# The first loads of a large matmul: two blocks of w issued by ScalarE, and one cast shared by two engines

## The chip, the core and the metric

The kernel runs on one core of one Trainium2 chip. A core has five engines, each with its own instruction stream: TensorE (PE in the profile; PEld is its weight load), VectorE (DVE), ScalarE (ACT), GpSimd (POOL) and SyncE (SP). Transfers between HBM and the core's memory are carried by 16 DMA engines; an engine only issues them, and a semaphore tells when one has landed. The metric is the time on the device in microseconds (us), lower is better.

## The reference

```python
B, S, D = 8, 2048, 2048          # x: [8, 2048, 2048] f32, w: [2048, 2048] f32
cs = np.cumsum(x, axis=1)
diff = cs - (cs shifted by one along axis 1, zeros first)
return np.matmul(diff, w).astype(np.float32)
```

The difference of a running sum is `x` again, so what must be computed is `x @ w`: 16384 x 2048 by 2048 x 2048, result in f32.

## The kernel before, in words

The 16384 rows of `x` are taken in 128 tiles of 128 rows. The first four tiles (`PLAIN = 4`) are multiplied in bf16, block by block, as `w` arrives from HBM; in this head of the kernel `w` is also measured (its largest values) and turned into scaled f16 blocks. All other tiles go in groups of four through products with sums and differences of these f16 blocks (fewer products, at the price of additions on VectorE and ScalarE). An order written out by hand (`ORDER`, `END_ORDER`) says how the steps of one group mix with those of the next. The change touches the head alone.

The order of each engine's instructions is fixed by the helper `after(engine, ask)`: what is asked for with it comes behind the last instruction so asked for on the same engine. DMAs issued in `fetch` and `load_x` are asked for directly, and follow the order of the code on SP's queue.

The head, step by step (line numbers are those of the profile):

- `w` is cut into 16 blocks of 128 rows (`ko` = 0 to 15) and two halves of 1024 columns (`h` = 0, 1). `fetch(h, ko)` (L257 to L259) loads one block of one half, 128x1024 f32, 512 KB. `load_x(q, rows)` (L223 to L228) loads a quarter of the columns of `x` (`q`), one tile of 128x512 f32, 256 KB, for each row tile in `rows`.
- The loop at L365 issues, all on SP: `x` rows 0 and 1 of quarter 0, block 0 of `w`, `x` rows 2 and 3, block 1, blocks 2 and 3, the four row tiles of quarter 1, blocks 4 to 7, and so on. Eight semaphores serve these loads in turn, so that a load waits until the one eight places before it has landed.
- `cast_x` (L235, VectorE) casts a pair of row tiles to bf16, 128x1024 at once. `turn_x` (L244, TensorE) transposes it in eight matmuls against a unit matrix into PSUM, and `turned` (L253 VectorE, L251 ScalarE) copies that to `xP`, from where TensorE takes it as weights.
- `cast(h, ko)` (L261 to L267) casts a block of `w` to bf16 into one of seven ring buffers `wb`. For the half `h = 0`, blocks below `EARLY = 2` are cast by ScalarE (L265); all others by VectorE (L267).
- `measure(h, ko)` (L273, ScalarE) takes the sum of absolute values of each row of a block.
- `plain(h, r, ko)` (L304) multiplies row tile `r` by a block: for `h = 0` two matmuls of 128x512 for each of the row tiles 0 to 2 and one for row tile 3, the left and then the right 512 columns of `wb`.
- `dummies` (L353) are matmuls of zeros into PSUM banks that are not yet in use. Eleven of them (`WARM`) stand first on TensorE, five and four more behind the two groups of transposes.

The sequence around the change is this (L371 to L380):

```python
        for a in range(2):
            xb = cast_x(0, [a])
            v = turn_x(xb, a, 6 + a)
            dummies([4 + i % 2 for i in range((5, 4)[a])])
            turned(0, a, v, "dve")
            if a == 0:
                for ko in range(EARLY):
                    cast(0, ko)
            for r in (2 * a, 2 * a + 1):
                plain(0, r, 0)
```

Behind it, blocks 1 to 15 follow: cast, measure, the seven matmuls; before every fourth block the next quarter of `x` is cast, transposed and copied. Then comes the second half of `w`, with the turning of `w` into f16 blocks beside it.

Of the kernel before, what the change touches and what calls it, by code (L numbers as in the profile page):

```python
# [10 lines left out]
def kernel(  # L11
# [6 lines left out]
    nc = tc.nc  # L18
    P = 128
# [6 lines left out]
    NH = N // 2  # L26
    NB = 512
# [15 lines left out]
    EARLY = 2  # L43
# [44 lines left out]
    def after(engine, ask):  # L88
        if engine in last:
            with tc.issue_after(last[engine].ins):  # L90
                said = ask()
        else:
            said = ask()
        last[engine] = said[-1] if isinstance(said, tuple) else said
        return said
# [90 lines left out]
    with ExitStack() as head:  # L186
# [4 lines left out]
        def turn_of(tiles):  # L191
            tiles.append(tiles.pop(0))
            return tiles[-1]
# [62 lines left out]

        def fetch(h, ko):  # L257
            wt = whole[ko % KH][:, ko // KH, h, :]
            nc.sync.dma_start(wt, w[ds(ko * P, P), ds(h * NH, NH)])  # L259

        def cast(h, ko):  # L261
            wt = whole[ko % KH][:, ko // KH, h, :]
            b = wb[h, ko] = turn_of(ring)
            if h == 0 and ko < EARLY:
                after("act", lambda: nc.scalar.copy(b, wt))  # L265
            else:
                after("dve", lambda: nc.vector.tensor_copy(b, wt))  # L267
# [14 lines left out]
        def taken(h, ko):  # L282
            cast(h, ko)
            measure(h, ko)
# [80 lines left out]
        for ko in range(KO):  # L365
            if ko in loads:
                load_x(loads[ko])
            if ko < 2:
                load_x(0, range(2 * ko, 2 * ko + 2))
            fetch(0, ko)  # L370
# [10 lines that stand above are left out]
        measure(0, 0)  # L381
        for ko in range(1, KO - 1):
            if ko >= EARLY:
                cast(0, ko)
            measure(0, ko)
            q = (ko + 1) // KQ
            turning = ko % KQ == KQ - 1
            if turning:
                xb = cast_x(q)
            for r in range(PLAIN):  # L390
                if turning and r in (0, PLAIN - 1):
                    a = r // 2
                    turned(q, a, turn_x(xb, a, 7), "act")
                plain(0, r, ko)
# [3 lines left out]
        for ko in range(AHEAD):  # L398
            fetch(1, ko)
            cast(1, ko)  # L400
# [15 lines left out]
        def bring(ko):  # L416
            fetch(1, ko)
            cast(1, ko)
            measure(1, ko)
            if ko == AHEAD:  # L420
                scale_of_w(0)
            if ko > AHEAD:
                turn_left(1)
            if ko == 10:
                load(PLAIN, 0)
                load(PLAIN, 1)
                weigh(PLAIN)
                scale_of(PLAIN)
            if ko == 11:
                narrow(PLAIN)  # L430
# [905 lines left out]
```

## Time and profile before

| | us |
|---|---|
| median of 3 runs | 1449.84 (1449.72 to 1450.08) |
| span of the profiled execution, first to last instruction | 1447.4 |
| TensorE busy (matmul) | 1437.9 (99%) |
| VectorE busy | 1319.0 (91%) |
| ScalarE busy | 970.5 (67%) |
| GpSimd busy | 43.8 (3%) |

The profiled execution's own time is known by its span alone, 1447.4 us; the timed runs take 2.4 us more than that. The granted clock of TensorE is full (1.000) over the span.

Rows of the profile are read like this. A row of a timeline gives start, duration, engine, line, operation, output <- input, shape and count; in square brackets stand the idle time of the engine just ahead, and what ended it (`<-DMA W<-in_w_dram`: a load into the tile `W` had landed). `SPq` is SP's queue of DMA issues. A row of the chain gives start, duration and what the chain was on at that time. A row of the waits gives who waited for whom: us in total, how many times, the longest. A row of the windows gives the stretch, its length, then for each engine busy time and count, the granted clock, the mean busy share of the 16 DMA engines (above 1 where transfers of one engine overlap), and GB/s. The head loads all its data into one tile, `W`, from `in_w_dram` and `in_x_dram`.

### The profile page before, as it was taken

What the parts mean: (1) busy time and instruction counts of PE and PEld (TensorE: products, weight loads), DVE (VectorE), ACT (ScalarE), POOL (GpSimd) and SP (SyncE); (2) the same over time, 40 slices, a digit from 0 to 9 for tenths busy, and PEclk for the clock granted to TensorE, in tenths of its full rate; (3) what the DMA queues carried; (4) which work ended last, traced back from release to release, by engine and by line L of the source; (5) the groups of instructions that cost most, each with busy time, mean ns of one, the idle gap of its engine ahead of it and who ended that gap; (6) DMA issues with size and microseconds to landing.
All of it is one profiled execution on the core that took longest, in us unless ns stands there. A gap on an engine that the chain in (4) does not pass through costs nothing.

```text
span 1447.4 us, 20191 instructions
## 1 busy us (share of the span) xinstructions
PE 1437.9 (99%) x6686; PEld 651.6 (45%) x6692; DVE 1319.0 (91%) x2310; ACT 970.5 (67%) x1472; POOL 43.8 (3%) x130
## 2 busy tenths in 40 slices
PE   8999999999999999999999999999999999999998
PEld 4444444444444444444444444444444444444443
DVE  4899899999999999999999999999999999999998
ACT  6987566666666776666666667666667766666662
POOL 0011000000000000000000000000000000000000
PEclk9999999999999999999999999999999999999999
DMA  9999788899888898888899888998878998889973
GB/s 363 368 257 298 200 234 232 239 253 253 226 224 239 238 254 245 231 233 236 248 247 232 234 238 233 262 240 234 228 234 240 252 234 239 226 242 248 255 200 127
DMA packets 378199, 351.58 MB, mean 243 GB/s; under 512 B 274800, under 2 KB 274800, under 8 KB 377968
## 3 DMA queue, kind: packets, MB, share of 16 engines
q1 hardware_dynamic: 378096, 350.31, 86.5%
q8 instruction: 52, 0.85, 0.2%
q14 instruction: 51, 0.42, 0.1%
HBM read 150.99 MB, written 134.22 MB: 197 GB/s over the span
## 4 chain that ended last, share of the span: by engine, by line
PE 97%; DMA 2%; DVE 0%; SPq 0%; issue 0%; DVEq 0%
PE b L628 62%; PE b L609 33%; PE b L304 2%; DMA W<-in_w_dram 2%; DMA W<-in_x_dram 0%; DVE c L639 0%; PE b L464 0%; SPq L225 0%; DVE wb L267 0%; SPq L259 0%; DVEq L267 0%; DVEq L639 0%
## 5 line engine op out<-in xcount | busy, mean ns | idle before, releaser
L639 DVE SCALAR_TENSOR_TENSOR c<-b,of,c 128x512 f32<-128x512 f32 x790 | 573.6, 746 | 71.1 <-PE b L628 61.4
L609 PE MATMUL b<-W,x 128*128 128x512 f16 x2144 | 507.1, 379 | 0.0
L636 ACT ACTIVATE c<-b,of 128x512 f32<-128x512 f32 x492 | 312.7, 680 | 220.2 <-PE b L628 113.8
L628 PE MATMUL b<-W,x 128*128 128x512 f16 x1904 | 454.9, 379 | 0.0
L164 ACT ACTIVATE F<-F,of 128x1024 f16<-128x1024 f32 x246 | 282.3, 1148 | 175.6 <-DVE of L144 173.4
L628 PEld LDWEIGHTS <-x 128*128 128x128 f16 x2500 | 244.6, 98 | 295.4 <-issue 1.0
L609 PEld LDWEIGHTS <-x 128*128 128x128 f16 x2144 | 209.7, 98 | 253.3 <-issue 0.5
L125 ACT ACTIVATE waste<-F 128x1024 uint8<-128x1024 f32 x246 | 259.3, 1054 | 8.3 <-DMA F<-in_x_dram 6.2
L628 PEld LDWEIGHTS <-inner 128*128 128x128 f16 x1644 | 160.8, 98 | 194.0
L628 PE MATMUL b<-W,inner 128*128 128x512 f16 x940 | 241.2, 379 | 0.0
L599 DVE TENSOR_TENSOR x<-x,x 128x1024 f16<-128x1024 f16 (+1 forms) x390 | 227.1, 583 | 3.3
L628 PE MATMUL b<-flow,x 128*128 128x512 f16 x584 | 149.9, 379 | 0.0
L628 PE MATMUL b<-inner 128*128 128x512 f16 x472 | 121.1, 379 | 0.0
L955 DVE TENSOR_TENSOR flow<-W 128x2048 f16<-128x2048 f16 x87 | 105.7, 1215 | 0.0
L1053 DVE TENSOR_TENSOR b<-b,c 128x512 f32<-128x512 f32 x116 | 80.4, 693 | 12.7 <-PE b L628 12.7
L150 POOL TENSOR_SCALAR of<-uw,of 128x2 f32<-128x2 f32 x124 | 42.6, 357 | 1299.6 <-DVE of L142 717.1
L955 DVE TENSOR_TENSOR flow<-W,inner 128x2048 f16<-128x2048 f16 x58 | 70.7, 1220 | 0.0
L1046 ACT COPY c<-b 128x512 f32<-128x512 f32 x58 | 33.4, 576 | 51.2 <-PE b L628 51.2
L304 PE MATMUL b<-wb,xP 128*128 128x512 bf16 x234 | 53.2, 379 | 2.2 <-ACT wb L265 1.1
L599 DVE TENSOR_TENSOR inner<-x 128x512 f16<-128x512 f16 x117 | 49.3, 421 | 3.1 <-DMA x<-F 1.0
L1046 ACT COPY b<-b 128x512 f32<-128x512 f32 x87 | 51.2, 589 | 0.2 <-PE b L628 0.2
L599 DVE TENSOR_TENSOR inner<-x,inner 128x512 f16<-128x512 f16 x117 | 49.2, 421 | 2.0
(68 smaller groups left out, 517.5 us busy)
## 6 DMA issues: line engine op xcount, KB each, us to landing
F<-in_x_dram SPq DMA_DIRECT2D x246, 512.0 KB, 5.2
out_dram<-c SPq DMA_DIRECT2D x492, 256.0 KB, 3.0
W<-in_w_dram SPq DMA_DIRECT2D x32, 512.0 KB, 8.4
W<-in_x_dram SPq DMA_DIRECT2D x16, 256.0 KB, 7.8
x<-F SPq DMA_TRANSPOSE x246, 3.4
out_dram<-o SPq DMA_DIRECT2D x5, 256.0 KB, 7.0
out_dram<-wb SPq DMA_DIRECT2D x5, 256.0 KB, 7.0
xP<-in_x_dram SPq DMA_DIRECT2D x1, 1024.0 KB, 6.4
```

What stands on the lines that cost most here:

```text
L125: lambda: nc.scalar.activation(waste, where[t][i], ABS, scale=1.0 / ROW, accum_out=sums_of[t][:, i : i + 1],),
L150: after("pool", lambda: nc.gpsimd.tensor_scalar(u, uw, m, None, MUL))
L164: lambda: nc.scalar.activation(narrowed(t)[:, ds(i * NH, NH)], where[t][i], COPY, scale=s),
L304: lambda: nc.tensor.matmul(ps[r][n], xP[:, r, ko, :], wb[h, ko][:, ds(n * NB, NB)], start=(ko == 0), stop=(ko == KO - 1),),
L599: after("dve", lambda: nc.vector.tensor_tensor(dst.all, p.all, q.all, op))
L609: said = nc.tensor.matmul(to[n], a[k], b[k][:, n, :], start=(first and k == 0), stop=(k == KH - 1), skip_group_check=True,)
L628: said = nc.tensor.matmul(to, a[k], b[k], start=(first and k == 0), stop=(k == 3), skip_group_check=True)
L636: after("act", lambda: nc.scalar.activation(c, p, COPY, scale=u))
L639: after("dve", lambda: nc.vector.scalar_tensor_tensor(c, p, u, c, MUL, ADD))
L955: after("dve", lambda: nc.vector.tensor_tensor(in_twos(to), x, y, op))
L1046: after("act", lambda: nc.scalar.copy(c, p))
L1053: after("dve", lambda: nc.vector.tensor_tensor(t, p, s, ADD))
```

## The change

Two things are changed in two helpers. `fetch` issues the first two blocks of the first half of `w` (`h == 0`, `ko < EARLY`) from ScalarE's queue instead of SP's; both come first in ScalarE's instruction stream. All other loads stay on SP, in their order. `cast` of the first block (`h == 0`, `ko == 0`) is cut by columns: VectorE casts the left 512, ScalarE the right 512. In VectorE's stream its half stands between the copy of the first pair of transposed row tiles and the cast of the second pair. Block 1 is still cast whole by ScalarE.

```diff
         def fetch(h, ko):
             wt = whole[ko % KH][:, ko // KH, h, :]
-            nc.sync.dma_start(wt, w[ds(ko * P, P), ds(h * NH, NH)])
+            if h == 0 and ko < EARLY:
+                after(
+                    "act",
+                    lambda: nc.scalar.dma_start(wt, w[ds(ko * P, P), ds(h * NH, NH)]),
+                )
+            else:
+                nc.sync.dma_start(wt, w[ds(ko * P, P), ds(h * NH, NH)])
 
         def cast(h, ko):
             wt = whole[ko % KH][:, ko // KH, h, :]
             b = wb[h, ko] = turn_of(ring)
-            if h == 0 and ko < EARLY:
+            if h == 0 and ko == 0:
+                sides = [ds(n * NB, NB) for n in range(2)]
+                after("dve", lambda: nc.vector.tensor_copy(b[:, sides[0]], wt[:, sides[0]]))
+                after("act", lambda: nc.scalar.copy(b[:, sides[1]], wt[:, sides[1]]))
+            elif h == 0 and ko < EARLY:
                 after("act", lambda: nc.scalar.copy(b, wt))
             else:
                 after("dve", lambda: nc.vector.tensor_copy(b, wt))
```

## The prediction

> **What bounds the kernel now.** I read the page first, then the chain that ended last for the first 45 us, then the timeline of each engine in the first 15 us, and last the windows for the rates of the DMA engines. The page:
>
> ```profile
> span 1447.4 us, 20191 instructions
> ...
> PE 97%; DMA 2%; DVE 0%; SPq 0%; issue 0%; DVEq 0%
> ```
>
> Nearly all of the span is TensorE's own work; 2% of the chain is DMA, and it lies at the start. The span is 1447.4 us, the median of the timed runs 1449.84 us; the 2.4 us between them lie around the span, and I carry them over unchanged. The chain in order of time shows where the DMA part is:
>
> ```profile
> 2.58 6.41 DMA W<-in_x_dram
> ...
> 9.01 7.81 DMA W<-in_w_dram
> ...
> 25.27 7.82 DMA W<-in_w_dram
> ...
> 33.21 0.71 DVE wb L267
> ...
> 33.96 8.16 PE b L304 x37
> ```
>
> From 2.58 to 33.2 us the chain is a ladder of loads: each rung is a load that SP could issue only when the one eight places before it had landed. From 33.96 us on it is TensorE alone. So the end moves by as much as the start of the piece at 33.96 us moves: this is the only place in which the change can earn or lose time, as long as TensorE has no waits of its own later. To move it, two things must both be early: block 12 of `w` (the cast at 33.21 us), and TensorE's work of blocks 0 to 11.
>
> The queue of SP, the only one that loads here:
>
> ```profile
> 0.72 0.87 SPq L225 DMA_DIRECT2D W<-in_x_dram  x2
> 1.65 0.42 SPq L259 DMA_DIRECT2D W<-in_w_dram  x1
> 2.11 0.91 SPq L225 DMA_DIRECT2D W<-in_x_dram  x2
> 3.06 2.29 SPq L259 DMA_DIRECT2D W<-in_w_dram  x3
> 5.39 3.28 SPq L225 DMA_DIRECT2D W<-in_x_dram  x4
> ```
>
> One issue takes about 0.46 us of SP (1.65 to 2.11). How the 16 DMA engines fare (the last two columns are their busy share and GB/s; the first numbers are the stretch and TensorE's busy time):
>
> ```profile
> 2.00:7.00 5.00, 4.37 (x21) 1.86 (x20) 2.29 (x7) 0.00 (x0) 0.00 (x0) 1.00 0.86 252
> ...
> 12.00:33.00 21.00, 19.23 (x114) 9.22 (x115) 10.68 (x16) 17.76 (x29) 0.00 (x0) 1.00 1.04 402
> 11.24:33.96 22.72, 20.88 (x127) 10.17 (x130) 11.80 (x17) 18.78 (x31) 0.00 (x0) 1.00 1.04 402
> ```
>
> In the steady part the engines are full: share 1.04, 402 GB/s. From 2 to 7 us they move 252 GB/s. That is a loss of 5.00 x (1 - 252/402) = 1.87 us of full-rate transfer, and the ladder carries it down to 33.2 us. It has two parts: the engines were less busy, 5.00 x (1 - 0.86/1.04) = 0.87 us, and while busy they moved less, the remaining 1.00 us.
>
> When the loads landed is seen from who waited for them. VectorE (pairs of `x` by L235, blocks of `w` by L267), then ScalarE (blocks 0 and 1 of `w`, L265):
>
> ```profile
> 5.17 0.69 DVE L235 CAST W<-W 128x1024 bf16<-128x1024 f32 x1 [1.91 <-DMA W<-in_x_dram]
> 6.58 0.69 DVE L253 COPY xP<-b 128x1024 bf16<-128x1024 bf16 x1 [0.72 <-PE b L244]
> 9.08 0.69 DVE L235 CAST W<-W 128x1024 bf16<-128x1024 f32 x1 [1.81 <-DMA W<-in_x_dram]
> 10.49 0.69 DVE L253 COPY xP<-b 128x1024 bf16<-128x1024 bf16 x1 [0.72 <-PE b L244]
> 11.57 0.69 DVE L267 CAST wb<-W 128x1024 bf16<-128x1024 f32 x1 [0.39 <-DMA W<-in_w_dram]
> 12.85 0.70 DVE L267 CAST wb<-W 128x1024 bf16<-128x1024 f32 x1 [0.58 <-DMA W<-in_w_dram]
> ```
>
> ```profile
> 0.72 1.28 ACT L265 ACT_TABLE_LOAD   x1 [0.72 <-PEq L1320]
> 7.67 1.04 ACT L265 CAST wb<-W 128x1024 bf16<-128x1024 f32 x1 [5.67 <-DMA W<-in_w_dram]
> 10.28 1.04 ACT L265 CAST wb<-W 128x1024 bf16<-128x1024 f32 x1 [1.57 <-DMA W<-in_w_dram]
> ```
>
> Each of these is 512 KB. They land at 5.17 (`x` rows 0 and 1), 7.67 (`w` 0), 9.08 (`x` rows 2 and 3), 10.28 (`w` 1), 11.57 and 12.85 us. The steady distance is 12.85 - 11.57 = 1.28 us; `w` 0 took 2.50 us behind the first pair. So the loss sits in the first pair and in `w` 0. TensorE in the same stretch:
>
> ```profile
> 1.17 4.11 PE L353 MATMUL b<-F 128*128 128x512 bf16 x11 [1.17 <-DVE F L207]
> 5.92 0.62 PE L244 MATMUL b<-eye,W 128*128 128x128 bf16 x8 [0.63 <-DVE W L235]
> 6.38 1.24 PE L353 MATMUL b<-F 128*128 128x512 bf16 x5
> 8.76 1.02 PE L304 MATMUL b<-wb,xP 128*128 128x512 bf16 x4 [1.14 <-ACT wb L265]
> 9.83 0.62 PE L244 MATMUL b<-eye,W 128*128 128x128 bf16 x8
> 10.29 1.03 PE L353 MATMUL b<-F 128*128 128x512 bf16 x4
> 11.24 1.47 PE L304 MATMUL b<-wb,xP 128*128 128x512 bf16 x6
> ```
>
> From 11.24 us on it has real work without fillers. Its waits between there and 33.96 us, in all:
>
> ```profile
> PE b L244 <- DVE W L235: 0.9, 2, 0.5
> PE b L304 <- DVE wb L267: 0.7, 1, 0.7
> ```
>
> That is 1.6 us (the window 11.24:33.96 above agrees: 22.72 - 20.88 = 1.84, dispatch gaps included). TensorE is thus nearly bound too: work that starts up to 1.6 us later than 11.24 us can still be caught up by 33.96 us, and if it does not start earlier, no more than 1.6 us can be won.
>
> **The change part by part.** *SP loses two issues.* The built program has SP issue the four `x` loads in a row, then blocks 2 and 3. At 0.46 us each, `x` rows 2 and 3 go out at about 1.65 and 2.11 instead of 2.11 and 2.58, and blocks 2 and 3 end at about 3.5 instead of 4.4 us.
>
> *ScalarE gains two issues*, ahead of its table load and of everything else. The trace shows no issue from ScalarE; the nearest rows are SP's 0.42 to 0.46 us, and I take 0.46. They would run from 0.72 to 1.6 us, and the table load to 2.9 us. Nothing on ScalarE wants to run before its first cast (7.67 us before), so this costs nothing; if that cover were gone, it would cost 0.9 us. `w` 0 goes out about 0.9 us sooner (1.65 to 0.72), `w` 1 about 1.9 us sooner (3.06 to 1.2).
>
> *The ladder's waits are renumbered.* The fifth to eighth `x` load now wait for `w` 0, `x` 0, `x` 1, `w` 1 to land, blocks 4 and 5 for `x` 2 and `x` 3. By 3.5 us 2.5 MB and more are in flight, over 6 us at 402 GB/s; SP's in-order wait for `w` 0 finds the engines with work for longer than `w` 0 can take (it landed at 7.67 us before, and it now leaves sooner). Cost nothing; if `w` 1 landed after 9 us, later rungs would slip by the excess.
>
> *The engines' start-up loss* is what decides. The trace shows no second queue at work, so I bound it by rows. At best all of the 1.87 us comes back: everything that was slow is waiting, and two queues wait beside each other. At worst nothing comes back, or `w` 1 takes as long as `w` 0 did: 2.50 - 1.28 = 1.22 us lost. I take the part in which the engines were not busy, 0.87 us: a second queue with a megabyte on offer fills empty time, while the slower transfer of busy engines need not change. This is the value near the middle of the ends, and nearest to a row.
>
> *The cast of `w` 0 is halved.* ScalarE's 1.04 us becomes about 0.57 (between half of it, 0.52, and the whole), VectorE gets one of about 0.4 us (between 0.35, half of 0.69, and 0.69). TensorE's first real matmul may come some 0.5 us sooner after `w` 0 has landed. But what follows at 9.83 us waits for the second pair of `x`, and what is late at 33.21 us is a load. Worth nothing at the end. What it adds is a wait: VectorE now stands at its half until `w` 0 has landed, and behind it are the cast of the second `x` pair and the second copy of L253. That costs only if `w` 0 lands after that pair, which the 0.9 us head start speaks against; then it would cost the difference.
>
> *After 33.96 us* the programs agree instruction for instruction on every engine, except for names and a few semaphore numbers. VectorE's, ScalarE's and SP's work there hangs on TensorE's or on loads of the same ladder, and moves with them.
>
> **Sum:** the loads reach block 12 0.87 us sooner. TensorE's start: with `x` sharing the engines with `w` I expect the first pair at about 6 us. From the pair's landing the rest is VectorE's and TensorE's chain: 2.10 us to the end of the first copy (5.17 to 6.58 + 0.69), 0.37 for VectorE's half, 0.69 for the second cast, and 1.45 to the first matmul behind the second copy, with 0.35 lost to TensorE's own order; about 5 us, so 11.0 us against 11.24. With 1.6 us of slack that suffices. 1449.84 - 0.87 = 1448.97, say 1449.0 us.
>
> **The rivals.** *Only the issue time.* The chain of the ladder starts behind SP's five issues; with one slot of 0.46 us less ahead of the last `x` load, it gains 0.46 us: 1449.4 us. For it: the engines' share of 0.86 leaves little room, and both queues feed the same engines. Against it: 252 GB/s is far from full. If the start-up loss were of the engines alone, even this goes and the time stays at 1449.8. [...] No run here shows two queues yet.
>
> *`x` starves behind `w` (slower).* If the engines serve both queues in turn, and a row of `w` is 4 KB against 2 KB of `x`, `w` gets two bytes for one of `x`. Were the total rate no better than before, the first pair of `x` would land with a megabyte of `w`, 1.5 MB in all, which had landed at 9.08 us before. Then the chain gives about 9.08 + 5.0 = 14.0 us for TensorE's start, 2.8 us later, of which 1.6 can be caught up: 1.2 us slower, 1451.0 us. It decides from a landing of the first pair at 7.9 us. TensorE would also idle from 5.28 to 9.8 us; were it to run the next stretch as slowly as its first eleven matmuls (4.11 us, against 11 x 0.25 = 2.7 by the 1.24 us for five), 1.4 us more: 1452.4. Against it: this needs the low total rate and the uneven share together; at 402 GB/s the pair lands by about 6. [...]
>
> *All of it comes back.* 1.87 us by the loads, but TensorE allows 1.6 and what its start gains: 1448.0 to 1448.2. For it: `w` 0 was slow while busy, and if that is a wait for first accesses it can overlap with `x`. Against: nothing in the trace shows overlap.
>
> **How the numbers follow.** Forecast (0.6 to 1.3 us gained) 0.42; issue time only or nothing (0 to 0.6) 0.23; all of it (1.3 and more) 0.15; `x` starves (0 to 3 us lost) 0.17; something else in the 1400 us behind, either way, 0.03. The likeliest gives 1449.0 us. The range takes in the first three and the near half of the fourth: 1447.8 to 1450.4. About 0.2%, 2.9 us, is what a measurement of this kernel can tell from no change; nearly every case is smaller than that. Faster by more needs more than the whole start-up loss: 0.02. Slower by more needs the starved `x` and the slow TensorE together: 0.04. Within: 0.94.
>
> **What would show it.** In the changed profile, the window 2 to 7 us should have a busy share near 1.0 and some 300 GB/s. The second pair's cast should start before 8.7 us, the cast of block 3 (12.85 us before) near 12.0, that of block 12 near 32.3, and TensorE's first matmul of the long unbroken piece (33.96 before) near 33.1, with nothing but this shift behind it. Wrong would be: a first pair after 7.9 us, a VectorE half that waits for `w` 0 while the second pair lies there, block 3 no sooner than 12.6, or a shift at 33 us that is gone by 130 us.

## The result, and the profile after

The changed kernel takes 1451.97 us (median of 21 runs, 1450.96 to 1452.72), the kernel before beside it 1449.56 us (21 runs). The ratio is 1.0016, with a 95% interval of 1.0009 to 1.0022: 2.4 us slower. The prediction was 0.9 us faster, with a range that ended at 1450.4 us; the time lies outside it. The profiled execution has a span of 1450.5 us (1447.4 before) and took 1452.44 us; it is one of the slower of the 21, so its span grows by 3.1 us where the medians differ by 2.4.

The timelines show what became of the loads. VectorE of the changed kernel, from the cast of the first pair of `x` on:

```profile
8.97 0.69 DVE L235 CAST W<-W 128x1024 bf16<-128x1024 f32 x1 [5.71 <-DMA W<-in_x_dram]
10.79 0.69 DVE L253 COPY xP<-b 128x1024 bf16<-128x1024 bf16 x1 [1.13 <-PE b L244]
11.40 0.42 DVE L272 CAST wb<-W 128x512 bf16<-128x512 f32 x1
11.73 0.68 DVE L235 CAST W<-W 128x1024 bf16<-128x1024 f32 x1
```

The first pair, which landed at 5.17 us before, now lands at 8.97 us. VectorE does not wait for `w` 0 at its half (no bracket at 11.40), nor for the second pair: both are there before it asks for them. ScalarE of the changed kernel shows why:

```profile
0.72 0.89 ACTq L262 DMA_DIRECT2D W<-in_w_dram  x2
1.64 1.28 ACT L273 ACT_TABLE_LOAD   x1 [1.64 <-PEq L1330]
6.88 0.62 ACT L273 CAST wb<-W 128x512 bf16<-128x512 f32 x1 [3.95 <-DMA W<-in_w_dram]
8.71 1.04 ACT L275 CAST wb<-W 128x1024 bf16<-128x1024 f32 x1 [1.21 <-DMA W<-in_w_dram]
```

Both blocks of `w` land ahead of the first pair: `w` 0 at 6.88 us (7.67 before) and `w` 1 at 8.71 us (10.28 before). TensorE can do nothing with them until `x` is there:

```profile
1.17 4.54 PE L363 MATMUL b<-F 128*128 128x512 bf16 x11 [1.17 <-DVE F L207]
9.72 1.03 PE L244 MATMUL b<-eye,W 128*128 128x128 bf16 x8 [4.01 <-DVE W L235]
10.55 2.34 PE L363 MATMUL b<-F 128*128 128x512 bf16 x5
12.68 1.91 PE L314 MATMUL b<-wb,xP 128*128 128x512 bf16 x4
14.39 1.06 PE L244 MATMUL b<-eye,W 128*128 128x128 bf16 x8
15.24 1.15 PE L363 MATMUL b<-F 128*128 128x512 bf16 x4
16.23 3.84 PE L314 MATMUL b<-wb,xP 128*128 128x512 bf16 x16
```

It idles for 4.01 us. What follows is slow: the five fillers take 2.34 us, 1.24 before; the four matmuls 1.91, 1.02 before. The first matmul behind the second copy comes at 16.23 us, 4.99 us later than the 11.24 of before. The windows (last three columns: granted clock, busy share of the DMA engines, GB/s) give the reason, and show the loads:

```profile
2.00:7.00 5.00, 3.71 (x10) 1.21 (x8) 1.18 (x5) 1.05 (x2) 0.00 (x0) 1.00 0.87 246
...
8.70:15.40 6.70, 5.68 (x26) 3.16 (x27) 2.32 (x4) 5.54 (x9) 0.00 (x0) 0.50 1.05 408
15.50:33.00 17.50, 17.34 (x102) 8.44 (x103) 11.21 (x18) 10.86 (x17) 0.00 (x0) 1.00 1.03 402
11.24:33.96 22.72, 22.56 (x122) 10.91 (x123) 13.02 (x21) 14.83 (x25) 0.00 (x0) 0.91 1.04 403
```

From 8.7 to 15.4 us the granted clock is 0.50. From 2 to 7 us the engines move 246 GB/s, not more than the 252 of before. And between 11.24 and 33.96 us TensorE now idles 22.72 - 22.56 = 0.16 us instead of 1.84: it has become the bound of the head. Of its 4.99 us it catches up about 2, and 3.1 us are left in the span (1450.5 - 1447.4). Which queue the engines served between 2 and 7 us is told by the profile's list of queues for that window alone (q10 is ScalarE's queue, q1 is SP's; packets, MB, share of the engines):

```profile
q10 hardware_dynamic: 225, 0.85, 57.5%
q1 hardware_dynamic: 203, 0.38, 29.0%
```

Nearly as many packets from one queue as from the other; but all but 34 of these packets are rows, 4 KB of `w` or 2 KB of `x`, so that `w` had 0.85 MB and `x` 0.38 MB, less than the 0.52 MB of its first pair. The landings, by the increments of the loads' semaphores, a few hundredths ahead of the casts above, say the same: `w` 0 landed at 6.85 us and row tile 0 of `x`, issued beside it, at 7.03; `w` 1 at 8.68 and row tile 1 at 8.87. Each row tile of `x` came in together with a whole block of `w`, and so the first pair with both blocks.

### The profile page after: what moved, and what is told of

Read it like the earlier page. It is cut to its first block, busy times and chain, and to the rows that moved or that the text cites. A ratio compares the mean times of both kernels' runs of the same rounds, so it can differ in the third digit from the quotient of the medians.

```text
span 1450.5 us, 20193 instructions
## 1 busy us (share of the span) xinstructions
PE 1440.3 (99%) x6686; PEld 653.3 (45%) x6692; DVE 1317.9 (91%) x2311; ACT 969.9 (67%) x1472; POOL 43.8 (3%) x130
## 4 chain that ended last, share of the span: by engine, by line
PE 95%; issue 1%; ACT 1%; DMA 1%; DVE 1%; SPq 0%; POOL 0%; DVEq 0%; ACTq 0%
PE b L638 61%; PE b L619 31%; PE b L314 1%; ACT waste L283 1%; DMA W<-in_x_dram 1%; DMA out_dram<-wb 1%; DVE W L352 0%; PE b L244 0%; DVE c L649 0%; PE b L363 0%; SPq L324 0%; ACT inner L646 0%; DVE x L344 0%; DVE wb L344 0%; ACT xP L164 0%
```

## The experiments

My theory after the result: the two queues move nearly as many packets as each other (225 to 203 above), so the two loads of `w`, with the longer rows, take two thirds of what the engines move (0.85 of 1.23 MB) and hold back the first pair; TensorE idles (4.01 us), its clock falls by half (0.50 from 8.7 to 15.4 us), and it starts its long run of work later than it can catch up (16.23 us against 11.24). The rivals: VectorE's new wait at its half of the cast; the late pair alone, without the clock; the clock alone; a cost of the second queue itself. Each time below stands beside that of the kernel before on the same chip.

**The cast halved, all loads on SP.** (This diff is against the kernel before; `fetch` stays as it was.)

```diff
-            if h == 0 and ko < EARLY:
+            if h == 0 and ko == 0:
+                sides = [ds(n * NB, NB) for n in range(2)]
+                after("dve", lambda: nc.vector.tensor_copy(b[:, sides[0]], wt[:, sides[0]]))
+                after("act", lambda: nc.scalar.copy(b[:, sides[1]], wt[:, sides[1]]))
+            elif h == 0 and ko < EARLY:
```

> The cast of block 0 halved, all loads on SP as before. Theory (the shared DMA engines hold back the first x pair, TensorE idles 4.0 us and its clock falls): nothing of that happens here; first pair's cast at 5.2 us, clock 1.00 throughout, time within 0.2 us of before (1449.6). Rival (VectorE's wait at its half, ahead of the second x pair, is what costs): the second pair's cast slips and 1 us or more of the 2.4 us lost shows here, 1450.6 or more.

Measured: 1449.55 us against 1449.46, ratio 1.0000 (0.9991 to 1.0008). VectorE of this kernel:

```profile
5.12 0.69 DVE L235 CAST W<-W 128x1024 bf16<-128x1024 f32 x1 [1.86 <-DMA W<-in_x_dram]
...
7.82 0.43 DVE L266 CAST wb<-W 128x512 bf16<-128x512 f32 x1 [0.60 <-DMA W<-in_w_dram]
9.22 0.69 DVE L235 CAST W<-W 128x1024 bf16<-128x1024 f32 x1 [0.97 <-DMA W<-in_x_dram]
```

It waits 0.60 us at its half and is done well before the second pair lands. The first real matmul comes at 8.30 instead of 8.76 us, and the end does not move: the cast is worth nothing, and its wait costs nothing. That rival is out.

**The two loads on ScalarE's queue, the cast whole.** The other half of the diff, alone.

> The two loads on ScalarE's queue, the cast of block 0 whole on ScalarE as before. Theory (shared engines and the clock): the first pair's cast at about 9.0 us, clock 0.5 in a stretch behind it, time as the changed kernel, 1451.5 to 1452.5. Rival (VectorE's wait at its half): most of the loss is gone, 1450.0 or less.

Measured: 1451.91 us against 1449.46, ratio 1.0017 (1.0008 to 1.0025). VectorE of this kernel:

```profile
9.01 0.69 DVE L235 CAST W<-W 128x1024 bf16<-128x1024 f32 x1 [5.76 <-DMA W<-in_x_dram]
```

The first pair lands at 9.01 us, TensorE idles 4.41 us. All of the loss comes with the queue.

**More filler matmuls ahead, so that TensorE does not idle.**

```diff
-    WARM = 11
+    WARM = 28
```

> The changed kernel with 28 instead of 11 filler matmuls at the start, so that TensorE works until about 9.4 us while it waits for the first x pair (9.0 us). Theory (late pair and clock both cost): the clock stays 1.00, the first matmul behind the second copy comes at about 14.0 instead of 16.3 us, 2.8 us later than before, of which 2.2 us are caught up: about 1450.2 (1449.8 to 1450.8). Rival (the late pair alone costs, the clock was absorbed): as the changed kernel, 1451.5 or more. Second rival (the clock alone costs): as before, 1449.6.

Measured: 1450.01 us against 1449.46, ratio 1.0005 (0.9996 to 1.0014), though the first pair landed later still (9.62 us). The granted clock is 1.00 in the windows from 2 to 33 us. TensorE of this kernel:

```profile
1.17 8.71 PE L363 MATMUL b<-F 128*128 128x512 bf16 x28 [1.17 <-DVE F L207]
10.37 0.62 PE L244 MATMUL b<-eye,W 128*128 128x128 bf16 x8 [0.49 <-DVE W L235]
10.83 1.24 PE L363 MATMUL b<-F 128*128 128x512 bf16 x5
12.11 1.02 PE L314 MATMUL b<-wb,xP 128*128 128x512 bf16 x4
12.97 0.61 PE L244 MATMUL b<-eye,W 128*128 128x128 bf16 x8
13.41 1.03 PE L363 MATMUL b<-F 128*128 128x512 bf16 x4
14.36 2.98 PE L314 MATMUL b<-wb,xP 128*128 128x512 bf16 x13
```

The same work from the transposes on takes 14.36 - 10.37 = 3.99 us, against 16.23 - 9.72 = 6.51 in the changed kernel. The changed kernel lost 2.41 us (1451.97 - 1449.56), this one 0.55: by the medians some 1.9 us come with the slow clock, and about half a microsecond with the late pair. The rival in which the late pair alone costs is out. The one in which the clock alone costs is not quite, since the interval takes in no loss; but all eleven times of this kernel (1449.59 us and more) lie above the median of the kernel before, and the last experiment, with the clock held too, has an interval above 1.

**The two blocks loaded in halves, with rows of 2 KB.**

```diff
-                after(
-                    "act",
-                    lambda: nc.scalar.dma_start(wt, w[ds(ko * P, P), ds(h * NH, NH)]),
-                )
+                for n in range(2):
+                    after(
+                        "act",
+                        lambda: nc.scalar.dma_start(
+                            wt[:, ds(n * NB, NB)], w[ds(ko * P, P), ds(h * NH + n * NB, NB)]
+                        ),
+                    )
```

> The changed kernel, but ScalarE loads each of the two blocks as two loads of 512 columns: rows of 2 KB, as those of x, same bytes. Theory (the engines serve the two queues turn by turn, one row each, so that 4 KB rows of w take two thirds): now one byte of w for one of x, the first pair lands with 0.5 MB of w instead of 1 MB, 1.5 to 2 us sooner, at about 7.0 us; idle under 2 us, clock 1.00, 1449.4 to 1450.0. Rival (the order in which the loads are queued or their bytes decide, not the rows): first pair at 8.5 us or later, time as the changed kernel, 1451.5 or more.

Measured: 1452.00 us against 1449.46, ratio 1.0017 (1.0008 to 1.0026); the first pair at 8.89 us. In time that is the rival's number. The queues between 2 and 7 us:

```profile
q1 hardware_dynamic: 293, 0.55, 44.2%
q10 hardware_dynamic: 314, 0.58, 40.7%
```

The share is what the theory said: 314 packets to 293, and now 0.58 MB to 0.55. But the engines moved only 225 GB/s, and VectorE's cast of the first pair, at 8.89 us, came behind the last of the 16 increments, as many as there are engines, of its second load (8.79 us); the increments of the two semaphores of the first pair, in us:

```
x row tile 0: 4.58 4.61 4.80 4.94 5.01 5.27 5.45 5.47 5.51 5.53 5.54 5.63 5.64 5.65 5.70 5.80
x row tile 1: 6.12 6.30 6.53 6.64 6.72 6.84 6.93 6.97 7.04 7.47 7.61 7.62 7.67 7.71 8.56 8.79
```

Row tile 0 is there at 5.80 us, 1.2 us sooner than in the changed kernel (7.03). Of row tile 1 fourteen engines were done by 7.71 us (8.56 in the changed kernel), but the last two came 0.9 and 1.1 us behind, as late as there (8.87). So in these two kernels the share went with the rows (0.85 MB to 0.38 with 4 KB rows of `w`, 0.58 to 0.55 with 2 KB), and 2 KB rows did not cure the late pair; why two engines fell behind stays open. This edit changes one thing more: with four loads on ScalarE's queue the first eight loads take all eight semaphores, so that SP issues block 2 of `w` only at 5.65 us (3.18 in the changed kernel).

**The x loads first, all on SP.** The changed kernel's order on SP, with `w` 0 and `w` 1 behind the four loads of `x` on the same queue (`fetch` is that of the kernel before; the diff shows the order alone).

```diff
-            if ko < 2:
-                load_x(0, range(2 * ko, 2 * ko + 2))
+            if ko == 0:
+                load_x(0)
```

> The changed kernel with its two loads of w back on SP, behind the four x loads: the order of the changed kernel's SP queue, one queue, the cast halved. Theory (it is the second queue beside x that holds back the first pair): first pair's cast at 5.2 us as before, second pair near 6.7, w 0 near 9.1, clock 1.00; TensorE's start behind the second copy near 12.2 us, within what can be caught up: 1449.4 to 1449.9. Rival (any order with w 0 behind the x loads and VectorE's wait costs): 1450.5 or more.

Measured: 1449.88 us against 1449.35, ratio 1.0004 (0.9995 to 1.0013). The first pair lands at 4.89 us (8.97 in the changed kernel), so it is the queue beside it that held it back. What this order makes late is `w` 0, and in the profiled execution the clock falls here as well. TensorE of this kernel, and its window:

```profile
10.53 1.02 PE L308 MATMUL b<-wb,xP 128*128 128x512 bf16 x4 [3.18 <-DVE wb L266]
```

```profile
12.00:33.00 21.00, 20.84 (x116) 9.99 (x118) 11.68 (x17) 17.57 (x28) 0.00 (x0) 0.92 1.04 402
```

An idle time of 3.18 us is followed by a mean clock of 0.92 over 21 us: 21 x 0.08 / 0.5 = 3.4 us at half speed. I had expected the clock to hold, `w` 0 near 9.1 and TensorE's start at 12.2 us; `w` 0 landed at 10.05 us, and the start was at 13.56. Fourteen engines were done with `w` 0 by 8.96 us; the last two came at 10.01 and 10.03. Whether the clock falls in every run of this kernel is not shown: six of eleven have a mean clock of 1.000 and take 1449.29 to 1449.88 us, as expected; five have 0.999 and take 1450.34 to 1450.69 us, the profiled one among them. One stretch of 3.4 us at half speed would make such a difference in the mean (3.4 x 0.5 / 1448.5 = 0.0012), but the mean alone does not tell it: 11 of the 22 runs of the kernel before beside it have 0.999 too, at 1449.12 to 1449.70 us.

**Only block 0 on ScalarE's queue.** (`ko == 0` in place of `ko < EARLY` in `fetch`.)

> The changed kernel with block 0 alone on ScalarE's queue, block 1 on SP behind the x loads. Theory (x waits for the w bytes that are offered beside it): the first pair lands with 0.5 MB of w, about 1 MB in all, which landed at 7.7 us before: its cast at 7.0 to 8.0 us, TensorE idle 2 to 3 us, and the time between: 1449.6 if the clock holds, up to 1451.5 if it falls. Rival (a second queue slows the start whatever it carries): first pair near 9.0 us, 1451.9.

Measured: 1450.42 us against 1449.35, ratio 1.0008 (0.9999 to 1.0017). VectorE of this kernel:

```profile
7.79 0.69 DVE L235 CAST W<-W 128x1024 bf16<-128x1024 f32 x1 [4.53 <-DMA W<-in_x_dram]
```

Half the `w` beside it, and the first pair lands well before the 8.97 us of the changed kernel, at 7.79 us; the idle time is 3.12 us, and the window from 7 to 12 us has a clock of 0.66, again 3.4 us at half speed. In these two kernels the delay of the pair against the 5.17 us of before goes with the bytes on the second queue (2.62 us with 0.5 MB, 3.80 us with 1 MB), not with there being one. (The interval of the time just takes in no loss.)

**The two loads on ScalarE's queue, issued only when the first pair has landed.** (In `fetch`, ahead of the issue.)

```diff
+                if ko == 0:
+                    pair = resting(KH - 1, 0)
+                    after("act", lambda: nc.scalar.copy(waste[:, :2], pair[:, NB - 1 : NB + 1]))
```

> The changed kernel, but ScalarE reads two columns of the landed first x pair before it issues its two loads, so that they can't run beside that pair. Theory (only the race with the first pair costs): first pair's cast at 5.2 us or sooner, no long idle, clock 1.00, w 0 near 8 to 9 us, time 1449.3 to 1450.0. Rival (ScalarE's queue costs by itself, with its waits on SP's ladder): 1451 or more.

Measured: 1454.01 us against 1449.35, ratio 1.0030 (1.0018 to 1.0041). Here I was wrong by 4 us. ScalarE's queue, VectorE and TensorE of this kernel:

```profile
4.97 1.39 ACTq L265 DMA_DIRECT2D W<-in_w_dram  x2
```

```profile
4.94 0.70 DVE L235 CAST W<-W 128x1024 bf16<-128x1024 f32 x1 [1.69 <-DMA W<-in_x_dram]
...
12.92 0.43 DVE L275 CAST wb<-W 128x512 bf16<-128x512 f32 x1 [5.88 <-DMA W<-in_w_dram]
```

```profile
13.40 1.87 PE L317 MATMUL b<-wb,xP 128*128 128x512 bf16 x4 [6.01 <-DVE wb L275]
```

The first pair is not held back (4.94 us), as expected. But now `w` 0, issued at about 5 us, lands at 12.92 us. It gets no share at first: from 2 to 7 us the list of queues has SP's alone,

```profile
q1 hardware_dynamic: 621, 1.27, 84.7%
```

and the first packet of ScalarE's queue starts at 8.88 us, 3.9 us after the issue. Row tiles 2 and 3 of `x` and blocks 2 and 3 of `w`, which SP had queued before, go ahead of it (block 3's increments come at 8.79 to 10.70 us); only then do the two queues run beside each other (from 11 to 13 us 147 packets of ScalarE's queue to 160 of SP's). I had counted the race for the first pair alone, and not what lies ahead of `w` 0 by then. Why the queue moved nothing for so long is not shown; so the rival, that ScalarE's queue costs by itself, is ruled out for loads that are issued first (by the kernel with block 0 alone on it), not for this case. TensorE idles 6.01 us and runs slowly until 18.7 us (the granted clock is 0.84 from 12 to 33 us).

**All loads later.** The kernel before; the first load of `x` has to wait for six fills of its tile, and the others queue behind it. (The diff is shown in part: the loads are also asked for with `after`, so that they keep their order on SP.)

```diff
+        for _ in range(6):
+            nc.vector.memset(resting(KH - 1, 0), 0.0)
-    WARM = 11
+    WARM = 28
```

> The kernel before with all loads held back by six fills of the first pair's tile on VectorE, and 28 filler matmuls: the first load is issued some 4 us later; nothing else is changed. It asks why the engines move only 250 GB/s in the first 5 us of loads. If that comes with the first loads (whenever they are issued), the distance between first issue and the second pair's cast stays 8.4 us (0.72 to 9.08), w 0 again takes about 2.5 us behind the first pair, and the time grows by all of the delay that TensorE can't catch up. If it comes with the start of the program (the clock on the wall), the loads run at about 400 GB/s from the first, the distance falls to 6.5 us or less and w 0 takes 1.3 us.

Measured, in a single run: 1458.05 us. The first load is issued at 9.48 us, 8.76 us later than before and not some 4. SP, VectorE and ScalarE of this kernel:

```profile
9.48 0.87 SPq L227 DMA_DIRECT2D W<-in_x_dram  x2
```

```profile
13.96 0.69 DVE L238 CAST W<-W 128x1024 bf16<-128x1024 f32 x1 [4.50 <-DMA W<-in_x_dram]
...
17.86 0.69 DVE L238 CAST W<-W 128x1024 bf16<-128x1024 f32 x1 [1.38 <-DMA W<-in_x_dram]
```

```profile
16.46 1.04 ACT L268 CAST wb<-W 128x1024 bf16<-128x1024 f32 x1 [14.46 <-DMA W<-in_w_dram]
```

From the first issue to the cast of the first pair it takes 13.96 - 9.48 = 4.48 us (4.45 before), to that of the second pair 8.38 us (8.36 before), and `w` 0 takes 2.50 us behind the first pair, as before. In this run the slow start came with the first loads, 8.76 us later than before.

**A small load of w ahead.** The kernel before, with 16 columns of block 0 loaded first on ScalarE's queue.

```diff
+        after("act", lambda: nc.scalar.dma_start(touch, w[:P, :16]))
```

> The kernel before, with one small load more: 16 columns of the 128 rows of block 0 of w (64 bytes a row) into a tile of its own, first on ScalarE's queue; all else as before. It asks why w 0 takes 2.5 us behind the first x pair when the blocks behind it take 1.28. If it is the first access to w, the small load takes that wait on itself beside x, w 0 takes 1.3 to 1.6 us, the second pair's cast starts before 8.3 instead of 9.08 us, and the loads of the whole head come up to 1.2 us sooner: 1448.3 to 1449.0. If not (a loss of the first bytes whatever they are), w 0 still takes about 2.5 us and the time is as before, 1449.2 to 1449.8.

Measured: 1450.03 us against 1449.64, ratio 1.0001 (0.9992 to 1.0010). `w` 0 lands at 7.49 us, 2.30 behind the first pair (5.19), the second pair at 8.89: 0.2 us sooner, not 1.2. A first access to these rows, of 64 bytes each, is not what makes `w` 0 slow.

**No filler matmuls ahead.** The kernel before with `WARM = 0`.

> The kernel before without its eleven filler matmuls ahead of the first transposes: TensorE starts at 5.9 us with its clock not yet released, all loads as before. It asks what a slow TensorE alone costs in the head. By the theory (a late start of the long run of real matmuls costs only what exceeds some 2 us) the first matmul behind the second copy slips by 1 to 3 us, and the time by 0 to 1 us: 1449.4 to 1450.4, although TensorE runs slowly for 3 to 7 us as in the changed kernel. Rival (the slow stretch costs what it takes, half of its length): 1451 or more.

Measured: 1449.97 us against 1449.64, ratio 1.0001 (0.9992 to 1.0010). TensorE is as slow as in the changed kernel up to 10.8 us, and its first matmul behind the second copy comes at 12.26 us, 1.02 later:

```profile
7.10 2.34 PE L353 MATMUL b<-F 128*128 128x512 bf16 x5
9.23 1.80 PE L304 MATMUL b<-wb,xP 128*128 128x512 bf16 x4
10.87 0.61 PE L244 MATMUL b<-eye,W 128*128 128x128 bf16 x8
11.31 1.03 PE L353 MATMUL b<-F 128*128 128x512 bf16 x4
12.26 3.84 PE L304 MATMUL b<-wb,xP 128*128 128x512 bf16 x17
```

The column of the granted clock reads 1.00 here from 2 us on all the same: it counts as full what has no record, and the trace has no record of the clock before 10.78 us (before 4.38 us in the kernel before, whose first eleven matmuls are slow too: 4.11 us, where five take 1.24 later). The durations show it. Here a slow TensorE cost nothing that can be told: its start slipped by 1.02 us, less than the 1.2 to 2.0 us that the loads leave it by the table below. In the changed kernel the slow matmuls come on top of the late pair, with a slip of 4.99 us in all.

**Rows of 2 KB and more fillers together.** (The halves above with `WARM = 28`.)

> The loads of w on ScalarE's queue in halves (2 KB rows) and 28 filler matmuls: the two remedies together. Theory (the slow TensorE behind the idle is most of the loss, and the loss of loads by itself is caught up): the clock stays 1.00, TensorE's first matmul behind the second copy at 12.5 to 14.3 us whether the first pair lands at 7.0 (the even share) or again near 8.9 us (the last of the 16 engines), and the time is 1449.6 to 1450.3. Rival (the second queue costs beyond TensorE's late start): 1451 or more.

Measured: 1450.76 us against 1449.41, ratio 1.0011 (1.0002 to 1.0020). The clock holds (1.00 in the windows from 2 to 33 us), the first pair lands at 8.54 us, TensorE's start is at 14.00 us, inside what was expected; the time is 0.5 us over the expected range, and 1.2 us under that of the halves without the fillers. The fillers themselves are part of it: they run until 10.18 us (1.17 + 9.01), and the transposes behind them start at 10.02 us, some 0.7 us later than the pair's landing would allow (0.75 us from cast to transposes in the changed kernel, 8.97 to 9.72).

Set side by side, with the start of TensorE's long run (first matmul behind the second copy, 11.24 us before) and the growth of the profiled span (1447.4 us before; one execution each, within 0.7 us of the growth of the medians):

| kernel | start, us | later by | span grows by |
|---|---|---|---|
| no fillers ahead | 12.26 | 1.0 | 0.3 |
| x first, on SP | 13.56 | 2.3 | 1.1 |
| only block 0 | 13.75 | 2.5 | 0.7 |
| halves, 28 fillers | 14.00 | 2.8 | 1.4 |
| 28 fillers | 14.36 | 3.1 | 1.2 |
| halves | 15.94 | 4.7 | 2.7 |
| changed kernel | 16.23 | 5.0 | 3.1 |
| issued after the pair | 17.62 | 6.4 | 4.8 |

From 2 us on, the span grows by the slip less 1.2 to 2.0 us, what the loads leave to catch up.

## Why the prediction was wrong, point by point

- **The engines' start-up loss** is the step that failed first. I took the 0.87 us in which the engines were not busy to come back, because "a second queue with a megabyte on offer fills empty time". It did not: with two queues the engines moved 246 GB/s from 2 to 7 us, with one 252, and 223 to 261 in all the kernels that load from the start. The loss belongs to the first loads (4.48 and 8.38 us behind the first issue, and the same when that is 8.76 us later). What makes them slow stays open; more on offer was no cure, and a first access to the rows of `w` is not the cause (2.30 us from the pair to `w` 0 with it taken ahead, 2.50 before). By the prediction's own sum this step alone would have left the time at 1449.8 us.
- **The first pair at about 6 us** failed with it, and this made the kernel slower: the pair landed at 8.97 us, because the loads of `w` beside it took two bytes for one (0.85 MB to 0.38). I had the price of this in the rival in which `x` starves behind `w`: the same share, no better total rate, a landing at 9.08 us. Both of its conditions held (0.85 MB to 0.38 MB, 246 GB/s), and I had given it 0.17 because it needed both. They were not two lucky throws: the low rate was measured, and only my hope for the second queue spoke against its staying. The range did not even fit this rival: its own price, 1451.0 us without a slow TensorE, lay above the range's end of 1450.4, while I gave 0.04 to anything slower and asked for the starved `x` and the slow TensorE together. The share that the rival gave `w` showed in the packets of loads that were issued together: 225 of one queue to 203 of the other, 314 to 293 with 2 KB rows. Row tile 0 of `x` landed 0.18 us behind `w` 0 (7.03 and 6.85 us), less than the 0.65 us that its 0.26 MB take at 402 GB/s, so the one load did not wait for the end of the other. For the loads issued at 5 us it did not hold (no packet until 8.88 us).
- **TensorE's start and the slack of 1.6 us**: the chain of about 5 us from the pair's landing gave 14.0 us, and with the clock held (28 fillers) it took 14.36 - 9.62 = 4.7 us. The slack held as well: 1.2 to 2.0 us. The rival's 1.2 us of loss is 0.55 us with the clock held (1.35 with rows of 2 KB, the fillers' own delay in it).
- **The slow clock** I priced at 1.4 us and made an afterthought of that rival. By the medians it is some 1.9 us of the 2.4, and 1.2 of 2.5 with rows of 2 KB. The traces show no fall after the idle time of 1.14 us in the kernel before, 6.8 us at half speed after 4.01 us in the changed kernel, and 3.4 us at half speed after 3.12 us (only block 0) and 3.18 us (`x` first). In the changed kernel the records of the clock are 3.41 us full (from 5.24 us), 6.83 us at half (from 8.66 us), then full to 1449.08 us. In the 3.41 us ahead of the fall TensorE was busy for 0.47 us there, for 0.78 us with block 0 only (from 4.64 us) and for 1.28 us with `x` first (from 8.39 us); in the kernel before, from 5.34 to 8.75 us, for 1.70 us, and the clock held. So the clock also fell where TensorE had not been idle throughout; what decides it beyond these figures is not shown. The prediction had the idle time in this rival (5.28 to 9.8 us), and did not ask what it alone does.
- **SP's two issues less**: right for `x` rows 2 and 3 (at 1.67 and 2.15 us), too large for blocks 2 and 3, which were issued by 4.56 us and not 3.5. Without effect: what all of them then waited for was the engines (busy share 1.03, 406 GB/s from 7 to 12 us).
- **ScalarE's two issues**: right. They took 0.89 us, the table load ran behind them, nothing waited.
- **The ladder's new waits**: right, no cost. Block 12's cast was at 32.92 us (33.21 before, 32.3 forecast), and by the profile it no longer waited for its load but for TensorE.
- **The halved cast**: right, nothing (1449.55 against 1449.46 us), and VectorE's wait at its half cost nothing.
- **After 33.96 us**: right. TensorE has the same busy time from 33 to 60 us (26.82 us of 27.00) in both, and what was lost by 34 us is lost at the end.

## What to carry to other kernels

In these runs a second queue did not add to what the DMA engines move at the start (246 GB/s against 252); it changed what landed first. Two queues whose loads were issued together moved nearly as many packets as each other (225 to 203), and the load with the longer rows pushed aside the one that everything waited for (8.97 us in place of 5.17); loads issued later, at 4.97 us, moved nothing until 8.88 us, behind what the other queue already had. Before loads are spread over queues, ask which landing the chain hangs on, and leave that load alone on the engines, but look at what then comes late in its place. And ask of every idle time that a change makes on TensorE whether it is long enough to lower the clock (here 3.12 us was, and 1.14 us was not): a start 3.1 us late cost about half a microsecond while the clock held, and some 2.4 us with the slow matmuls on top. No version that I tried was faster than the kernel before.

## What the runs showed of the hardware that was not expected

- The first loads of the kernel are slow in the same way when they are issued 8.76 us later (one run): 4.45 and 4.48 us to the first 0.5 MB, 2.50 us for the next 0.5 MB, against 1.28 us later on; one queue or two, 223 to 261 GB/s against 402.
- Two queues whose loads were issued together moved nearly as many packets as each other from 2 to 7 us: 225 to 203 in the changed kernel, which with rows of 4 KB and 2 KB gave 0.85 and 0.38 MB, and 314 to 293 with 2 KB rows. With block 0 alone on ScalarE's queue it was 132 to 381, 0.48 MB of the block's 0.52 and 0.71 MB. A load issued on the second queue at 4.97 us, behind six loads of the first queue that had not landed, moved nothing until 8.88 us.
- After idle times of 3.12 us (only block 0) and 3.18 us (`x` loads first) TensorE's granted clock was 0.5 for 3.4 us, after 4.01 us (changed kernel) for 6.83 us, and after 4.27 to 6.01 us (four other kernels) for 6.8 to 7.0 us by the clocks of the windows. By the trace's records of the clock the slow stretch began 2.9 us after the idle time had begun in the changed kernel (8.66 us), and 4.5 us after in the kernel with the `x` loads first (11.81 us), where TensorE was already at work again. In the kernel with the `x` loads first five of eleven runs, the profiled one among them, took 1450.34 to 1450.69 us, six 1449.29 to 1449.88 us.
- What waited for a load began behind the last increment of its 16 engines (rows of 2 KB: 8.79 us, the cast at 8.89). At the start the last two came up to 2.3 us behind the fourteenth (row tile 3 of `x` with the `x` loads first: 6.42 us, then 8.72 and 8.73).
